# One step of a hybrid encoder layer on one core: the second value pair formed plainly, token squares moved back, roots spread in steps, and sliding-window attention fed from the last gate product

## The chip, the core and the metric

The kernel runs on 1 core of one Trainium2 chip. The metric is device time in microseconds (us), the median of several runs. TensorE (PE) does the matmuls, VectorE (DVE), ScalarE (ACT) and GpSimd (POOL) the elementwise work, and SyncE (SP) issues most of the DMAs. Each engine takes its instructions in the order in which the program lists them.

## The reference, cut to what matters

One layer is computed for 1024 prompt frames and 64 sample frames, here side by side as 1088 columns of 1024 features. With `xn = rms_norm(x)`:

```
rq, rk, rv, rg, sq, sk, sv, ga, gb = split(xn @ w_in)
q, k = rope(rq), rope(rk) / 16                       # 4 heads of 256
for chunk of 64:                                     # retention
    s = (q @ k.T) * decay;  o = s @ v + (q @ state) * q_dec
    state = state * gamma**64 + (k * k_dec).T @ v
a = (rms_norm(o) * silu(rg)) @ w_ret_out
p = softmax(sq @ sk.T / 8 + bias, with a sink)       # 16 heads of 64, window 192
b = (p @ sv) @ w_swa_out
x += (sigmoid(ga) * a + sigmoid(gb) * b) @ w_mix_out
x += cross_attention(rms_norm(x), memory keys and values)
x += (silu(hn @ w_gate) * (hn @ w_up)) @ w_down      # hn = rms_norm(x)
y = rms_norm(x)
```

Everything is float32. A product of two float32 matrices is formed in three matmuls of a reduced float type (`fp32r`): high times high, high times low, low times high. So each operand is split into a high part (ACT casts it, L125) and a low part (DVE subtracts, L126).

## The kernel before, in words

**Projection stage (`project_phase`).** The columns of `w_in` are handled in pairs of 256. The 1024x1088 operand is cut into four quarters B11, B12, B21, B22 (features by tokens), and a pair of weight blocks likewise into a11, a12, a21, a22. `strassen` forms the pair's result in 7 products, P1, P2, P6, P5, P7, P3, P4 in this order, with the operands B11, B21, T2, T1, T3, B22, T4, where T1 to T4 are differences of the quarters. `plain` and `plain_columns` form it in 8 products of the quarters themselves. A product is 24 matmuls of 128x272 columns (`multiply`, L209 to L212). It fills one of three PSUM bank pairs (`pq`), which come round in turn, and a bank pair is free again when its result has been read: by ACT (`u1`, L273, or a copy, L644) or by DVE (`u2`, `u3`, `u5`, L270; the result `stage`, L646). `weight_ops` forms the seven weight operands of a pair from two raw tiles; POOL does its sums (L186 to L193), for the second pair DVE. The weight operands go round in five buffers (`wq`).

**The start.** The first value pair is formed by `plain`, because T1 to T4 do not exist yet. The second value pair is formed by `strassen`, whose T operands DVE and ACT prepare meanwhile (`start_phase`, L484 to L502). Then come keys and queries of head 0, `rotated(w_k, 0)` and `rotated(w_q, 0)`: each result is turned by the rotary table `rope` on DVE (L677 to L683). `token_squares` loads x once more in 16 tiles `xsq` through four buffers (L513), squares them on ACT (L514) and adds them up on DVE (L516). The buffers of `rope` and `xsq` lie where the start's tiles (`early`, `w`) lay.

**Retention beside it.** From `rotated(w_k, 1)` on, one step of the generator `retention_steps` is put behind every product (`product`, `step`). The fourth step forms the token roots (L525 and the chain from L307), a later one spreads them over all partitions (`spread_roots`: nine small matmuls L536 into two banks, three ACT copies L538, all in one step). After that each head takes 25 steps. The pieces wait on each other in PE's order (`in_order`).

**Gates and memory keys.** Twelve gate pairs follow: four of `w_ga`, four of `w_rg`, four of `w_gb`. The first three lie beside the last retention steps. From the fourth on steps of `memory_phase` lie behind each pair.

**Sliding-window attention (SWA, `mix_phase`, `swa`).** 17 chunks of 64 tokens, each in two halves of 8 heads. For a half: `scores` (4 matmuls, L1100), the softmax on DVE and ACT (L1110 to L1126) and POOL (L1128), `turn` (transposes of the probabilities, L1143 and L1151, and a copy by ACT, L1145, and one by DVE, L1153) and `weigh` (4 full and 4 tail matmuls, L1166 and L1171). Step i holds `weigh` of half i-1, `scores` of half i+2, `turn` of half i, and then pieces from `filler`: memory values of heads 2 and 3 (8 pieces), then the product with `w_ret_out` in 8 rows of blocks by 3 column chunks of 384, 384 and 320 (48 pieces of 12 matmuls, L152 to L154). The product's operands `ret` are the gated retention outputs; they are loaded from `d_gate` into the tiles `swin` and split (L125, L126). All of this stage's inputs are loaded when the last gate product has been issued, and `ret` of all three column chunks is split at the stage's beginning:

```
head, (c0, n) = [], CH[0]
...
for t, groups in zip(self.chunk, (((0, 1), (4, 5), (6,)), ((7,), (2, 3)))):
...
operands(head[:5], *CH[0], first)
...
operands(fetch(*CH[t + 1]), *CH[t + 1], (self.max_done, self.exp_done))
```

**What sets the order.** A scheduler puts the instructions of each engine in order; `issue_after` and `in_order` keep an instruction behind another in that order. An engine does not pass over an instruction that waits, and SP does not pass over a DMA that waits.

Of the kernel before, what the change touches and what calls it, by code (L numbers as in the profile page):

```python
# [11 lines left out]
F32 = mybir.dt.float32  # L12
# [4 lines left out]
PSUM = bass.MemoryType.PSUM  # L17
# [93 lines left out]
class Kernel:  # L111
# [57 lines left out]
    def weight_ops(self, raws, n=512, skip=(), by=None):  # L169
# [13 lines left out]
        tt = (by or nc.gpsimd).tensor_tensor  # L183
# [8 lines left out]
        self.ready = self.last_cast, self.last_low  # L192
# [229 lines left out]
    def start_phase(self, ctx):  # L422
# [57 lines left out]
        with tc.issue_after(behind[0]), tc.issue_after(behind[1]):  # L480
            self.second = self.weight_ops(self.load_raws([io["w_v"][2 + i] for i in range(2)]), by=nc.vector)
# [5 lines left out]
        with tc.issue_after(self.ready[0]), tc.issue_after(self.ready[1]):  # L487
# [14 lines left out]
        self.sums_done = self.last_low  # L502
# [27 lines left out]
    def spread_roots(self):  # L530

        for c0, n in ((0, 512), (512, 512), (1024, SMP)):
# [5 lines left out]
            self.nc.scalar.copy(self.rstd[:, c0:c0 + n], pb[:, :n])  # L538

# [74 lines left out]
    def project_phase(self):  # L614
        nc, tc, io = self.nc, self.tc, self.io
        with ExitStack() as ctx:
# [108 lines left out]
            first = self.second  # L725
            sctx.close()
            stage, long, count = *self.stage_tiles(), [0]
            with ExitStack() as rctx:
# [20 lines left out]
                for m in (0, 2, 4):  # L749
# [6 lines left out]
            steps = [0, 1, 2, 2, 2, 3, 3, 2, 0]  # L756
            for idx, w, act in ((1, "w_ga", AF.Sigmoid), (0, "w_rg", AF.Silu), (2, "w_gb", AF.Sigmoid)):
                for m in range(6 if idx == 1 else 0, KT, 2):
# [7 lines left out]
            raws = [self.unit_raw(io["w_mv"][2, i], 4, 256) for i in range(2)]  # L766
            self.values_loaded = self.loaded
            self.value_units = [self.unit_parts(raw, 4, 256) for raw in raws]
# [10 lines left out]
    def retention_steps(self):  # L779
# [6 lines left out]
        self.spread_roots()  # L786
        yield
# [36 lines left out]
    def retention(self, h):  # L824
# [107 lines left out]
        yield  # L932
        pss = self.bank("psss")
# [73 lines left out]

# [29 lines left out]
    def swa(self, ctx, fill):  # L1037
        nc, tc, io = self.nc, self.tc, self.io
        if True:
# [4 lines left out]
            flat = [t.rearrange("p a b -> p (a b)") for t in self.ring_tiles(0, KT, "swin", F32)]  # L1044
# [7 lines left out]
            self.lds += [t[:, i * 384:(i + 1) * 384] for t in (flat[6], flat[3]) for i in range(5)]  # L1052
            self.chunk = [flat[6][:, :5 * 384], flat[3][:, :3 * 384]]
            with tc.high_priority():
                def tokens(dst, i, cache):
                    self.load(dst[:, :SEQ], self.d_skv[i, :, :SEQ])
                    self.load(dst[:, SEQ:SEQ + P], io[cache])
                    ins = self.load(dst[:, SEQ + P:], self.d_skv[i, :, SEQ:])
                    return ins

                tokens(kT, 0, "ckT")
                self.load_queries(qTs, 0)
            with tc.high_priority(), tc.issue_after(self.values_loaded):
                self.bias_loaded = self.load(bias, self.d_bias)
# [67 lines left out]
            def turn(c, hf):  # L1132
                ks, j0, nk = keys(c)
                wide = nk == NKEY
                if hf == 0:
                    tail = [values(ks + P), values(ks - 64)] if wide else None
                    live[c] = [values(ks + 64) if wide and i else values(ks) for i in range(2)], tail
                t = live.pop((c, hf))
                n = min(P, nk)
                pp = pw.tile([P, 512], F32, tag="pt0", name="pp")  # L1140
# [3 lines left out]
                pT = sw.tile([P, 512], F32, tag="pT0", bufs=2, name="pT")  # L1144
                nc.scalar.copy(pT[:n, :], pp[:n, :])  # L1145
                rT = None
# [729 lines left out]
```

## Time and profile before

| | |
|---|---|
| median of 3 runs | 2233.99 us (2232.12 to 2236.03) |
| profiled execution, its own time | 2237.74 us |
| its span from first to last instruction | 2235.7 us |
| mean granted TensorE clock | 0.989 |
| busy: PE, DVE, ACT, POOL | 2166.8, 1605.8, 881.7, 703.6 us |

The page of the profile gives busy times of the engines over the span; "windows" give the same for a stretch of it, with the TensorE clock that was granted there (1.00 is full speed); the chain and the waits name what released an instruction that waited. Start times in the timeline are from the span's start. "x24" behind a row counts instructions; a float32 matmul that is not fp32r counts twice.

### The profile page before, as it was taken

How to read it: one execution, taken by the hardware profiler on the slowest of the kernel's cores; microseconds unless marked ns; L12 is line 12 of the kernel's file. 1: busy time of each engine (PE TensorE's matmuls, PEld its weight loads, DVE VectorE, ACT ScalarE, POOL GpSimd, SP SyncE). 2: the span in 40 equal slices, each digit the busy share in tenths (PEclk: the TensorE clock that was granted, in tenths of full speed). 3: DMA queues.
4: the chain of work that ended last, by engine and by line, in shares of the span. 5: the costliest groups of instructions: out<-in, count | busy, mean ns of one | idle time of the engine just before them, and what ended most of it. 6: DMA issues, size and time to landing. Idle time of an engine off the chain costs nothing.

```text
span 2235.7 us, 42154 instructions
## 1 busy us (share of the span) xinstructions
PE 2166.8 (97%) x16620; PEld 2117.3 (95%) x16620; DVE 1605.8 (72%) x2697; ACT 881.7 (39%) x1897; POOL 703.6 (31%) x522
## 2 busy tenths in 40 slices
PE   9899999999999999999999999999999999999987
PEld 8899999999999997889999998999999999999987
DVE  7888878667688667885455555659777776779787
ACT  6334343436444356553133333324223222335433
POOL 0223535253254112220000000015555555434561
PEclk9999999999999999999999999999999999999999
DMA  6423433344444566326443112422342333476332
GB/s 213 138 98 118 143 118 123 112 146 124 156 142 166 158 237 207 115 71 210 129 153 106 56 48 65 134 85 84 132 135 91 102 116 94 129 246 202 119 120 81
DMA packets 160456, 291.90 MB, mean 131 GB/s; under 512 B 21539, under 2 KB 89059, under 8 KB 160131
## 3 DMA queue, kind: packets, MB, share of 16 engines
q1 hardware_dynamic: 151122, 263.97, 36.8%
q0 software_dynamic: 5104, 17.44, 2.1%
q10 hardware_dynamic: 4032, 7.80, 1.0%
q8 instruction: 131, 2.15, 0.4%
q14 instruction: 67, 0.54, 0.1%
HBM read 197.99 MB, written 91.95 MB: 130 GB/s over the span
## 4 chain that ended last, share of the span: by engine, by line
PE 74%; DVE 10%; DMA 6%; POOL 3%; issue 3%; ACT 3%; SPq 0%; DVEq 0%; ACTq 0%; POOLq 0%
PE pq L209 14%; PE pq L212 14%; PE pq L210 13%; PE pd L152 7%; PE pd L153 7%; PE pd L154 7%; DVE wq L126 3%; PE pss L1100 1%; DVE T L126 1%; DMA hl<-d_op 1%; DVE B L126 1%; DMA xsq<-xT 1%; PE pout L1166 1%; ACT wq L125 1%; POOL raw L189 1%
## 5 line engine op out<-in xcount | busy, mean ns | idle before, releaser
L126 DVE TENSOR_TENSOR wq<-raw,wq 128x512 fp32r<-128x512 f32 (+1 forms) x505 | 459.7, 915 | 154.5 <-ACT wq L125 152.2
L125 ACT CAST wq<-raw 128x512 fp32r<-128x512 f32 (+1 forms) x505 | 305.2, 613 | 602.5 <-PE pq L212 248.3
L209 PE MATMUL pq<-T,wq 128*128 128x272 f32 x1832 | 505.3, 293 | 20.1 <-DVE stage L646 7.8
L210 PE MATMUL pq<-T,wq 128*128 128x272 f32 x1832 | 499.8, 289 | 0.8 <-DVE T L126 0.7
L209 PE MATMUL pq<-B,wq 128*128 128x272 f32 x1526 | 419.3, 292 | 0.5 <-DVE u L270 0.5
L210 PE MATMUL pq<-B,wq 128*128 128x272 f32 x1526 | 414.9, 289 | 0.9 <-DVE B L126 0.9
L212 PE MATMUL pq<-T,wq 128*128 128x272 f32 x1832 | 380.7, 289 | 0.8 <-DVE wq L126 0.8
L186 POOL TENSOR_TENSOR raw<-raw 128x512 f32<-128x512 f32 (+1 forms) x58 | 81.6, 1406 | 939.7 <-DVE rs_r L309 485.9
L209 PEld LDWEIGHTS pq<-T,wq 128*128 128x128 f32 x1832 | 347.6, 190 | 23.3 <-issue 9.0
L210 PEld LDWEIGHTS pq<-T,wq 128*128 128x128 f32 x1832 | 350.9, 192 | 1.5 <-DVE T L126 1.5
L212 PE MATMUL pq<-B,wq 128*128 128x272 f32 x1526 | 316.6, 288 | 0.0
L210 PEld LDWEIGHTS pq<-B,wq 128*128 128x128 f32 x1526 | 291.4, 191 | 1.3 <-DVE B L126 1.3
L209 PEld LDWEIGHTS pq<-B,wq 128*128 128x128 f32 x1526 | 288.6, 189 | 1.4 <-ACT wq L125 0.7
L212 PEld LDWEIGHTS pq<-T,wq 128*128 128x128 f32 x1832 | 286.2, 189 | 1.1 <-DVE wq L126 1.0
L212 PEld LDWEIGHTS pq<-B,wq 128*128 128x128 f32 x1526 | 237.6, 189 | 0.0
L270 DVE TENSOR_TENSOR u<-pq,u 128x544 f32<-128x544 f32 x177 | 127.0, 718 | 79.1 <-PE pq L212 78.3
L189 POOL TENSOR_TENSOR raw<-raw 128x512 f32<-128x512 f32 (+1 forms) x58 | 83.1, 1432 | 117.5 <-DVE wq L126 117.5
L646 DVE TENSOR_TENSOR stage<-pq,u 128x544 f32<-128x544 f32 x112 | 80.1, 716 | 43.0 <-PE pq L212 22.8
L1128 POOL TENSOR_TENSOR t<-t,den 128x768 f32<-128x768 f32 (+2 forms) x34 | 47.7, 1403 | 137.8 <-DVE den L1126 61.1
L193 POOL TENSOR_TENSOR raw<-raw 128x512 f32<-128x512 f32 (+1 forms) x58 | 85.6, 1476 | 16.1 <-DVE wq L126 12.5
L187 POOL TENSOR_TENSOR raw<-raw 128x512 f32<-128x512 f32 (+1 forms) x58 | 83.8, 1444 | 3.7
L1658 POOL TENSOR_TENSOR y<-u,y 128x544 f32<-128x544 f32 x38 | 62.1, 1647 | 49.7 <-DVE y L1656 29.3
(404 smaller groups left out, 4762.5 us busy)
## 6 DMA issues: line engine op xcount, KB each, us to landing
hl<-d_op SPq DMA_DIRECT2D x84, 272.0 KB, 4.0
d_op<-stage SPq DMA_DIRECT2D x44, 272.0 KB, 2.2
d_op<-ht SPq DMA_DIRECT2D x44, 272.0 KB, 4.0
raw<-w_gate SPq DMA_DIRECT2D x22, 512.0 KB, 3.5
raw<-w_up SPq DMA_DIRECT2D x22, 512.0 KB, 4.7
raw<-w_down SPq DMA_DIRECT2D x16, 512.0 KB, 3.9
d_qkv<-stage SPq DMA_DIRECT2D x28, 272.0 KB, 2.4
d_gate<-stage ACTq DMA_DIRECT2D x28, 272.0 KB, 2.5
```

The lines of the kernel that those rows point to most:

```text
L125: self.last_cast = self.nc.scalar.copy(hi, src).ins
L126: self.last_low = self.nc.vector.tensor_tensor(out=lo, in0=src, in1=hi.bitcast(F32), op=ALU.subtract).ins
L152: mm(ps, wh, xh, start=start, stop=False)
L153: mm(ps, wh, xl, start=False, stop=False)
L154: self.last_mm = mm(ps, wl, xh, start=False, stop=stop).ins
L187: tt(out=a21, in0=a21, in1=a22, op=add)
L189: tt(out=a11, in0=a22, in1=a11, op=sub)
L193: self.last_sum = tt(out=a12, in0=a12, in1=a11, op=sub).ins
L209: mm(ps[:, c, :HC], w[:, 0, ks], x[:, 0, cs], start=start, stop=False)
L210: mm(ps[:, c, :HC], w[:, 0, ks], x[:, 1, cs], start=False, stop=False)
L212: self.last_mm = mm(ps[:, c, :HC], w[:, 1, ks], x[:, 0, c * HC:(c + 1) * HC], start=False, stop=stop).ins
L270: add = lambda out, a, b: nc.vector.tensor_tensor(out=out, in0=a, in1=b, op=ALU.add)
```

## The change

1. **Second value pair.** Its weights are split plainly (`plain_weights`, 4 operands and no sums) and `plain_columns` forms it in 8 products, before the start's tiles are given up; its results go through `early` and not through `stage`.
2. **Squares later.** `token_squares` now comes behind the last cast and the last low part of T4, and its buffers become free only after the second pair.
3. **Roots in steps.** `spread_roots` yields after each of its three pieces, and retention's small sample part has one yield more, so that retention has 118 steps where it had 112. All four `w_ga` pairs now lie beside retention.
4. **SWA inputs behind the last gate pair's products.** `refill` calls `swa_inputs` after each product of the last `w_gb` pair: as soon as an operand's place is free, keys, queries, bias and the first 384 columns of the gated retention output are loaded, and these are split into `ret`, in the places of B21, T2, T3 and B22. Raw weights of the memory values are loaded there too.
5. **Other columns.** The 16 tiles of the other two column chunks are fetched into the places of the first ones, and split two at a time, at each piece of `filler`. The three first rows of blocks of `w_ret_out` go together (`lead=3`, before 2), and the outputs of `filler` go round in 4 places until the last of these tiles is split (before 12).
6. **Weighing.** `turn` writes both halves of a chunk into one tile (`tall`, `rest`, one buffer each), and `weigh` of a chunk is one set of 8 matmuls of 256 columns, at every second step, where it was two sets of 8 matmuls of 128 columns.
7. **PSUM.** The banks of the transposes get a pool of their own, ahead of the output's and the scores': transposes, output and scores now lie in the first, second and third bank pair of the projection, where it was output, scores and transposes.

```diff
-            self.second = self.weight_ops(self.load_raws([io["w_v"][2 + i] for i in range(2)]), by=nc.vector)
+            self.second = self.plain_weights(self.load_raws([io["w_v"][2 + i] for i in range(2)]))
...
-        self.sums_done = self.last_low
+        self.sums_done = self.last_cast, self.last_low
...
             self.nc.scalar.copy(self.rstd[:, c0:c0 + n], pb[:, :n])
+            yield
...
             values(first, 0, self.plain)
-            first = self.second
+            values(self.second, 1, self.plain_columns)
             sctx.close()
-            stage, long, count = *self.stage_tiles(), [0]
+            stage, long, count = *self.stage_tiles(), [4]
...
-                values(first, 1)
                 rotated(pair("w_k", 0), 0, 1)
-                with tc.issue_after(self.sums_done):
+                with tc.issue_after(self.sums_done[0]), tc.issue_after(self.sums_done[1]):
                     self.token_squares()
...
-                for m in (0, 2, 4):
+                for m in (0, 2, 4, 6):
                     gate_columns(1, "w_ga", AF.Sigmoid, m)
...
+                    if (idx, m) == (2, KT - 2):
+                        self.refill = self.swa_inputs(mp)
...
+        def split(name, ks):
+            ring, slots = self.slots[name]
+            for k, slot in zip(ks, slots):
+                t = self.rets[k] = self.rings[ring].tile(f"ret{k}", slot=slot)
+                a = dict(self.columns)[k]
+                self.split(a[:, :n], t[:, 0, c0:c0 + n], t[:, 1, c0:c0 + n])
...
+            if name == "B11":
...
+                kT = swin(0)[:, :KC]
+                self.tokens(kT, 0, "ckT")
...
+                columns(swin(6), ((0, 1), (4, 5), (6,)))
+            elif name == "T2":
+                split("B21", (0, 1))
+            elif name == "T1":
+                self.load(swin(2)[:, :NPAIR * NKEY].rearrange("p (a b) -> p a b", b=NKEY), self.d_bias)
+                columns(swin(3), ((7,), (2, 3)))
+                split("T2", (4, 5))
+            elif name == "B22":
+                self.value_units = [self.unit_parts(raw, 4, 256) for raw in raws]
+                split("T3", (6, 7))
+            elif name == "T4":
+                split("B22", (2, 3))
...
         nc.vector.tensor_scalar(kv[:SMP, 1, :], pv[:SMP, 0, :], self.rtok[:SMP, 8:], None, ALU.mult)
         yield
+        yield
...
-            self.po, self.pw = (ctx.enter_context(self.tc.tile_pool(name=n, bufs=1, reuse_waits="tile", space=PSUM))
-                                for n in ("pout", "pw"))
+            self.pt, self.po, self.pw = (ctx.enter_context(self.tc.tile_pool(name=n, bufs=1, reuse_waits="tile", space=PSUM))
+                                         for n in ("pturn", "pout", "pw"))
...
-                        self.last_mm = mm(po[rows[v], i, at], full[i][:n, rows[v]], pT[:n, j * P:(j + 1) * P],
-                                          start=True, stop=rT is None).ins
+                        self.last_mm = mm(po[rows[v], i, :2 * P], full[i][:n, rows[v]], row(tall[:n, 2 * v + i]),
+                                          start=True, stop=rest is None).ins
...
-                if i > 0:
-                    self.in_order(lambda: weigh(*halves[i - 1]))
+                if i > 0 and i % 2 == 0:
+                    self.in_order(lambda: weigh(i // 2 - 1))
...
-            for m, u, (c0, n) in self.m_major(units, CH, tail=1, lead=2):
+            for m, u, (c0, n) in self.m_major(units, CH, tail=1, lead=3):
...
                 for ps in self.pieces(u, rets, c0, n):
+                    if left:
+                        operands(2)
```

**Where instructions move.** The first place is DVE at the end of the second value pair and the beginning of `rotated(w_k, 0)`. `pq` is a product's result, `u` a partial sum of it, `stage` a result, `T_302` and `T_303` (after: `T_289` and `T_290`) are T4, `xsq` a tile of squares, `rope` the rotary table, and `wq<-raw` the low part of a weight operand. Before:

```order
L500 SCALAR_TENSOR_TENSOR xg_115<-xg_115,gains 128x544 x2
L500 SCALAR_TENSOR_TENSOR xg_116<-xg_116,gains 128x544 x2
L126 TENSOR_TENSOR T_302<-xg_115,T_302 128x544 x2
L126 TENSOR_TENSOR T_303<-xg_116,T_303 128x544
L270 TENSOR_TENSOR u_531<-pq,u_530 128x544
L126 TENSOR_TENSOR T_303<-xg_116,T_303 128x544
L516 TENSOR_TENSOR rstd<-rstd,xsq 128x544
L126 TENSOR_TENSOR wq<-raw,wq 128x512
L646 TENSOR_TENSOR stage_522<-pq,u_529 128x544
L646 TENSOR_TENSOR stage_522<-pq,u_532 128x544 x2
```

After, from the end of T4 on:

```order
L126 TENSOR_TENSOR T_290<-xg_116,T_290 128x544
L126 TENSOR_TENSOR wq<-raw,wq 128x512 x4
L646 TENSOR_TENSOR stage_714<-pq,u_749 128x544
L126 TENSOR_TENSOR wq<-raw,wq 128x512
L678 TENSOR_TENSOR stage_713<-stage_714,rope 128x544
L269 TENSOR_TENSOR u_750<-pq,u_749 128x544
L679 TENSOR_TENSOR stage_714<-stage_714,rope 128x544
L515 TENSOR_TENSOR rstd<-rstd,xsq 128x544
L269 TENSOR_TENSOR u_752<-pq,u_750 128x544
L515 TENSOR_TENSOR rstd<-rstd,xsq 128x544 x2
L126 TENSOR_TENSOR wq<-raw,wq 128x512 x2
L269 TENSOR_TENSOR u_751<-pq,u_750 128x544
```

No result of the second pair stands among the T operands any more, and a row that reads `rope` now stands ahead of the readings of the key product's banks, with the squares between them.

The second place is DVE in `rotated(w_q, 0)`, around its P2, which is the row `stage<-pq,u_1043` in both. Before:

```order
L126 TENSOR_TENSOR wq<-raw,wq 128x512
L646 TENSOR_TENSOR stage_523<-pq,u_1043 128x544
L270 TENSOR_TENSOR u_1044<-pq,u_1043 128x544
L678 TENSOR_TENSOR stage_522<-stage_523,rope 128x544
L126 TENSOR_TENSOR wq<-raw,wq 128x512
L679 TENSOR_TENSOR stage_523<-stage_523,rope 128x544
L270 TENSOR_TENSOR u_1046<-pq,u_1044 128x544
```

After:

```order
L515 TENSOR_TENSOR rstd<-rstd,xsq 128x544
L269 TENSOR_TENSOR u_1044<-pq,u_1043 128x544
L683 TENSOR_TENSOR stage_713<-stage_713 128x544
L515 TENSOR_TENSOR rstd<-rstd,xsq 128x544
L126 TENSOR_TENSOR wq<-raw,wq 128x512
L269 TENSOR_TENSOR u_1046<-pq,u_1044 128x544
L646 TENSOR_TENSOR stage_714<-pq,u_1043 128x544
```

The reading of P2's bank moved from ahead of the readings of P6 and P5 (`u_1044`, `u_1046`) to behind both, with squares among them.

The third place is ACT where SWA begins; `pT` is the copy of the transposed probabilities, `ret` the operands of the product with `w_ret_out`. Before:

```order
L1145 COPY pT<-pp 64x512
L125 CAST wq<-raw 128x512 x4
L1122 ACTIVATE t,den<-t,nm 128x128 x4
L1124 ACTIVATE es<-es 128x4
L125 CAST ret_9663<-swin_9628 128x320
L125 CAST ret_9664<-swin_9626 128x320
L125 CAST ret_9667<-swin_9632 128x320
L125 CAST ret_9668<-swin_9632 128x320
L125 CAST ret_9669<-swin_9632 128x320
L125 CAST ret_9670<-swin_9632 128x320
L125 CAST ret_9665<-swin_9632 128x320
L125 CAST ret_9666<-swin_9629 128x320
```

After:

```order
L1203 COPY pT<-pp 64x4x128
L1133 COPY swin_9672<-pd 128x128
L125 CAST wq<-raw 128x512 x2
L1177 ACTIVATE t,den<-t,nm 128x128 x4
L1179 ACTIVATE es<-es 128x4
L125 CAST ret_9489<-swin_9430 128x384
L125 CAST ret_9492<-swin_9430 128x384
L1203 COPY pT<-pp 64x4x128
```

The run of eight casts between one half's exponentials and the next copy has become a pair.

More of the change, by code (lines that the diff above doesn't have):

```diff
@@ L755, in project_phase @@
             memory = self.memory_phase(mp)
-            steps = [0, 1, 2, 2, 2, 3, 3, 2, 0]
-            for idx, w, act in ((1, "w_ga", AF.Sigmoid), (0, "w_rg", AF.Silu), (2, "w_gb", AF.Sigmoid)):
-                for m in range(6 if idx == 1 else 0, KT, 2):
+            steps = [1, 2, 2, 2, 3, 3, 2, 0]
+            for idx, w, act in ((0, "w_rg", AF.Silu), (2, "w_gb", AF.Sigmoid)):
+                for m in range(0, KT, 2):
+                    if (idx, m) == (2, KT - 2):
+                        self.refill = self.swa_inputs(mp)
                     with tc.issue_after(gate_columns(idx, w, act, m)):
@@ L785, in retention_steps @@
             yield
-        self.spread_roots()
-        yield
+        yield from self.spread_roots()
         for h in range(H):
@@ L1042, in swa @@
             mm = nc.tensor.matmul
-            flat = [t.rearrange("p a b -> p (a b)") for t in self.ring_tiles(0, KT, "swin", F32)]
+            for i in range(KT):
+                if i not in self.swin:
+                    self.swin[i] = self.rings[0].tile(f"swin{i}", F32, slot=(self.rings[0].next + i) % KT)
+            flat = [self.swin[i].rearrange("p a b -> p (a b)") for i in range(KT)]
             kT, vT = flat[0][:, :KC], flat[5][:, 64:64 + KC]
@@ L1051, in swa @@
             self.lds = [flat[2][:, NPAIR * NKEY:][:, :384], flat[0][:, KC + 3 * P:][:, :384]]
[L1052 to L1064, printed above, removed]
+            self.lds += [flat[3][:, i * 384:(i + 1) * 384] for i in (3, 4)]
+            with tc.high_priority(), tc.issue_after(self.raws_loaded):
+                self.tokens(vT, 1, "cvT")
+                self.load_rows(qTs[0], 2, 2)
             def keep():
@@ L1202, in swa @@
                         keep()
-            self.in_order(lambda: weigh(*halves[n - 1]))
+            self.in_order(lambda: weigh(n // 2 - 1))
             for pieces in next(fill):
@@ L1263, in filler @@
                     us = self.value_units
-                    first = self.max_done, self.exp_done
                 else:
-                    part = lambda i: self.unit_parts(raws[i // 2][:, i % 2 * 512:][:, :512], 2, 256)
-                    last = lambda: (self.last_cast, self.last_low)
                     with tc.issue_after(self.last_gate):
-                        us = sum((part(i) for i in range(3)), [])
-                    with tc.issue_after(last()[0]), tc.issue_after(last()[1]):
-                        operands(head[:5], *CH[0], first)
-                    with tc.issue_after(last()[0]), tc.issue_after(last()[1]):
-                        us += part(3)
-                    operands(head[5:], *CH[0], last())
-                    us = us[:4], us[4:]
+                        us = [self.unit_parts(raw, 4, 256) for raw in self.raws]
                 for t in range(2):
```

125 lines of the change are left out of this document (68 added, 57 removed).

## Prediction

> **What bounds the kernel now.** I read the page first, then the table of stages (windows), then PE's waits, and for the places the change touches the timeline. The page's first line and the stages that matter (length, then busy us and count of PE, weight loads, DVE, ACT, POOL, then PE's granted clock):
>
> ```profile
> PE 2166.8 (97%) x16620; PEld 2117.3 (95%) x16620; DVE 1605.8 (72%) x2697; ACT 881.7 (39%) x1897; POOL 703.6 (31%) x522
> 33.60:69.10 35.50, 25.84 (x171) 24.69 (x170) 33.63 (x49) 16.24 (x28) 5.50 (x4) 0.86 0.49 162
> 69.10:114.00 44.90, 42.78 (x337) 42.30 (x337) 37.18 (x52) 15.37 (x27) 11.26 (x7) 1.00 0.44 140
> 142.70:150.50 7.80, 7.80 (x51) 7.80 (x51) 7.15 (x12) 1.37 (x4) 0.00 (x0) 0.78 0.33 121
> 150.50:595.00 444.50, 434.14 (x3419) 425.19 (x3417) 340.21 (x609) 191.09 (x411) 174.17 (x151) 0.99 0.39 124
> 595.00:799.20 204.20, 204.20 (x1643) 204.13 (x1643) 148.41 (x199) 85.49 (x145) 76.00 (x62) 1.00 0.49 160
> 799.20:820.50 21.30, 21.27 (x170) 21.05 (x168) 11.86 (x18) 7.63 (x13) 4.11 (x5) 1.00 0.89 310
> 820.50:836.40 15.90, 13.99 (x121) 13.25 (x121) 11.89 (x30) 12.52 (x37) 1.43 (x4) 1.00 0.81 269
> 836.40:883.00 46.60, 40.55 (x292) 34.47 (x290) 35.21 (x90) 27.38 (x99) 10.38 (x8) 0.89 0.72 229
> ```
>
> PE is the bound; a gain is an idle stretch that goes, a low clock that goes, or matmuls that go. Before SWA's steady part there are three such places: the second value pair (33.6 to 69.1: 9.7 idle, clock 0.86, while DVE is busy 33.63 of 35.50), the roots, and the beginning of SWA (820.5 to 883: 1.9 and 6.1 idle, clock 0.89). Retention (150.5 to 595) has 10.4 idle. From 595 to 820.5, through the gates, PE has no gap worth the name, so nothing is to be had there. PE's waits say who ended the idle time (total us, times, longest):
>
> ```profile
> PE pq L209 <- DVE stage L646: 7.8, 3, 5.7
> PE po L152 <- DVE state L899: 3.3, 2, 2.4
> PE pb L536 <- ACT rstd L538: 3.2, 1, 3.2
> PE pout L1166 <- ACT pT L1145: 3.0, 1, 3.0
> PE pd L152 <- ACT swin L1284: 2.6, 1, 2.6
> PE pss L152 <- DVE kt L857: 2.5, 1, 2.5
> PE psss L935 <- DVE kvs L929: 2.3, 1, 2.3
> PE pb L979 <- ACT ret_o L969: 2.0, 1, 2.0
> PE pd L153 <- DVE wq L126: 1.1, 1, 1.1
> PE pss L1100 <- DVE stage L646: 0.8, 1, 0.8
> ```
>
> **Part 1: second pair, squares, first keys and queries.** A product's price comes from a stretch that holds one; the timeline rows are the pair's first matmul, its worst wait, and the first matmul of `rotated(w_k, 1)`:
>
> ```profile
> 814.30:817.32 3.02, 3.02 (x27) 3.02 (x26) 2.59 (x4) 0.83 (x2) 0.00 (x0) 1.00 1.03 368
> 33.65 0.29 PE L209 MATMUL pq<-B,wq 128*128 128x272 f32 x1
> 64.03 0.57 PE L209 MATMUL pq<-T,wq 128*128 128x272 f32 x1 [5.67 <-DVE stage L646]
> 114.00 0.29 PE L209 MATMUL pq<-B,wq 128*128 128x272 f32 x1
> ```
>
> A product is 3.02 us. Before, 21 products (7, 7 and 7) took 114.00 - 33.65 = 80.35 us. Now there are 22, one more at +3.02: 66.4 us without a wait, so 100.1, a gain of 13.9 at most. The second pair itself should run freely: its four weight operands need no sums, the quarters exist already, ACT reads its banks, and the T operands are due only with P6 of the keys, about 64. So the wait of 5.67 goes. What is late next is DVE's queue behind it. These rows are the loads behind the first pair's stores, the first square on ACT, the median landing of the stores and of the `xsq` loads, and DVE at full rate:
>
> ```profile
> 37.54 0.42 SPq L119 DMA_DIRECT2D rope<-c_rope  x1
> 38.01 2.15 SPq L119 DMA_DIRECT2D xsq<-xT  x4
> 46.28 0.66 ACT L514 ACTIVATE rstd<-xsq 128x544 f32<-128x544 f32 x1 [5.55 <-DMA xsq<-xT]
> xsq<-xT SPq DMA_DIRECT2D x16, 272.0 KB, 4.0
> d_qkv<-early SPq DMA_DIRECT2D x4, 272.0 KB, 2.4
> 39.61 5.16 DVE L126 TENSOR_TENSOR T<-xg,T 128x544 fp32r<-128x544 f32 x8
> ```
>
> `rope` and `xsq` lie over `early`, so on SP they now stand behind the second pair's last store: 33.65 + 8 x 3.02 = 57.8, a copy by ACT (0.6, as the copy in part 4) and two issues (0.4 each), 2.4 to land, so about 62. Before, the first square ran 8.3 us after its load was issued; so `rope` and squares are there at about 70. A row that reads `rope` stands in DVE's queue ahead of the keys' partial sums, and all the squares are still to come. From it to the reading of P2's bank in `rotated(w_q, 0)` the order has 39 instructions; at 5.16 / 8 = 0.645 us that is 25.2, so 95.2, and about 3 us of waiting for the fifth `xsq` tile, whose load stands behind a weight load that waits for DVE: 98. P7 needs this bank at 57.8 + 11 x 3.02 = 91.0. So PE waits about 7 there. Such gaps also cost clock: 0.14 x 35.5 = 5 us for the two large ones before, so 2 for this one. Gain: 13.9 - 7 - 2 = **5 us**. Ends: 13.9 if DVE keeps up, 0 if it waits twice as long. The clock row at 142.7 bears on a rule: in the Trainium skill, "TensorE: Matmul & The Clock Gate", Part 1: The HAM clock gate, PE falls to half clock only after an idle window of about 3.4 us. By that rule the gaps of under 3.4 us below would cost no clock, and the sum would be about 5 us smaller (1.7 in part 2, 3 in part 4); the trace disagrees, with 0.78 right behind a gap of 3.17.
>
> **Part 2: the roots.** The wait, in the timeline:
>
> ```profile
> 142.29 0.43 PE L536 MATMUL pb<-ident,rtok 64*128 64x64 f32 x2 [3.17 <-ACT rstd L538]
> ```
>
> The third piece waits for a bank that ACT empties; with a product between the pieces it doesn't. That gives 3.17, and 0.22 x 7.8 = 1.7 of clock: 4.9, taken as **4.5**; ends 0 and 4.9. The squares' last tiles land before this, since the roots come 18 products after the second pair.
>
> **Part 3: retention.** The additional yield puts a product between `kvs` and its matmul: 2.3 gone. Its other waits (2.4, 2.5, 2.0, and 0.9 within the 3.3) depend on which product each step meets, and every step now meets another one; I take them as they are: **2.5 us**, ends +10 (none left) and -8 (as many again). The three later spreads of 118 steps still end inside the 119 products beside them, and the fourth `w_ga` pair is only moved past pool boundaries.
>
> **Part 4: SWA's beginning.** ACT's rows show the reason of the 2.6 and 3.0 waits, casts of `ret` in bursts ahead of what PE waits for; the next two show the load of the second `w_ret_out` rows and the cast that waited for it, the last a whole step of SWA later on:
>
> ```profile
> 836.41 2.98 ACT L125 CAST ret<-swin 128x384 fp32r<-128x384 f32 x7
> 847.02 2.96 ACT L125 CAST ret<-swin 128x320 fp32r<-128x320 f32 x8
> 849.89 0.57 ACT L1145 COPY pT<-pp 64x512 f32<-64x512 f32 x1
> 836.49 0.42 SPq L119 DMA_DIRECT2D raw<-w_ret_out  x1
> 841.88 1.14 ACT L125 CAST wq<-raw 128x512 fp32r<-128x512 f32 x2 [0.58 <-DMA raw<-w_ret_out]
> 878.61:883.00 4.39, 4.39 (x44) 3.63 (x43) 3.07 (x7) 2.37 (x10) 1.47 (x1) 1.00 0.29 87
> ```
>
> The 24 splits cost the same, but eight move under the last gate pair, where DVE is busy 11.86 and ACT 7.63 of 21.30 and PE never waits, and sixteen go out in pairs. At 2.98 / 7 = 0.43 on ACT and no more than 0.645 on DVE the eight add 3.4 and 5.2 us there: covered; without cover each would hold up the reading of a bank by 0.645, 5 us in all. The 0.8 goes too, since the scores' banks are now those of P7, not of P4, which is read last. All of it is worth 1.9 + 6.1 idle and 0.11 x 46.6 = 5.1 of clock: 13. But in the new order a pair of `wq` casts stands ahead of the third half's exponentials, and the raw tile of the third rows is free only when the first rows are split. A load to its cast took 841.88 - 836.49 = 5.4 us, a step of PE lasts 4.4: I leave 3 us of wait and 2 of clock. Gain **8 us**; ends 2 and 13.
>
> **Part 5: weighing.** PE's groups in SWA's steady part (883 to 1005, 25 halves):
>
> ```profile
> L1166 PE MATMUL pout<-pT,swin 128*64 128x128 f32 x200 | 16.4, 285 | 0.0
> L1171 PE MATMUL pout<-rT,swin 64*64 64x128 f32 x200 | 11.2, 294 | 0.0
> L1100 PE MATMUL pss<-swin,swin 64*128 64x192 f32 x192 | 22.1, 349 | 0.0
> ```
>
> Columns are the same, instructions half. Per instruction: 82 ns at 128 columns (L1166), 115 at 192 (L1100), so 0.52 ns a column and 16 ns that don't depend on columns. A chunk loses 16 instructions: 0.26 us, times 17 is 4.4, taken as **4 us**; ends 0 (time goes by columns alone) and 8 (twice the fixed part). The single buffers cost nothing: the next `turn` stands behind `weigh` on PE anyway.
>
> **The sum.** 5 + 4.5 + 2.5 + 8 + 4 = 24 us. Against the profiled execution's 2237.74 (span 2235.7 and 2 around it) that is 2213.7. The median of the runs lies 3.75 below that execution, so the forecast is 2233.99 - 24 = **2210**.
>
> **The rivals.**
> *All waits go.* DVE keeps up because `rope` lands sooner, and the third weight load is in time: 9 and 5 us more, 38 in all, 2196. For it: DVE saves the second pair's sums and readings. Against: its queue is full as it is, 37.18 of 44.90.
> *The waits move.* Part 1 gives 0, part 4 gives 3, part 5 gives 1, with the roots' 4.5: 8.5, so 2225.5. For it: an engine's queue is in order, and new rows stand ahead of the readings in two of the three places shown.
> *Weighing gives nothing.* the 16 ns are hidden behind the matmul before, and time goes by columns alone: 0 instead of 4, so 2214. The groups speak against it with their 16 ns. It is what the Trainium skill says in "TensorE: Matmul & The Clock Gate", Back-to-back issue gap: a fixed part of about 2.5 ns for a matmul, by which 272 fewer would save 0.7 us; no row here shows a matmul with so small a part.
> *Nothing is left.* The wait in part 1 is 14 and SWA's beginning stays as it is: within 0.2%, about 2231.
> *Slower, by retention.* Every step behind the roots meets another product than before. In a product beside which DVE turns keys, a step's operand is 2.4 late (`state`, `kt`), and a gap costs about 1 of clock (0.01 x 444.5 over five gaps). At ten of the 16 blocks that is 34 us, against 21.5 from the other parts: +12.5, so 2246.5. It decides from eight blocks on. Against it: before, three blocks had such a gap.
>
> **How the numbers follow.** Chances: the forecast 0.48, all waits go 0.15, the waits move 0.16, weighing gives nothing 0.07, nothing is left 0.06, slower by retention 0.08. Faster by over 0.2% (4.5 us, about what a measurement of this kernel tells from no change): 0.48 + 0.15 + 0.16 + 0.07 = 0.86; same 0.06; slower 0.08. The range takes in the forecast's own spread and the two rivals around it, 2196 and 2225.5, with a little for their sizes: 2194 to 2228.
>
> **What would show it.** In the profile after: the second pair's 192 matmuls without a gap, at full clock, ending near 58; a wait of P7 in `rotated(w_q, 0)` for DVE's `stage`, and `rotated(w_k, 1)` beginning near 109; no wait of L537's spread; no `kvs` wait; scores right behind the last gate product, one wait of a few us for a `w_ret_out` load, and no low clock from 840 on the old scale; a weighing group of 100 instructions under 16.4 - 1 us. Wrong would be: more than eight waits of over 2 us in retention; or DVE's rows for `xsq` standing so late that the roots wait for them.

## The result, and the profile after

| | before | after |
|---|---|---|
| median of 4 runs | 2235.01 us | 2207.93 us (2206.57 to 2209.00) |
| ratio, 95% interval | | 0.9876 (0.9861 to 0.9890) |
| profiled execution | 2237.74 us | 2208.46 us |
| its span | 2235.7 us | 2206.7 us |

The change made the kernel 27.1 us faster; 24 were forecast. (Of the executions of the kernel before beside the first experiments below, one took 10017 us; it counts in no ratio.) The page's first line on the changed kernel:

```profile
PE 2156.8 (98%) x16388; PEld 2103.6 (95%) x16388; DVE 1591.5 (72%) x2683; ACT 882.6 (40%) x1899; POOL 713.9 (32%) x522
```

Its windows over the stages that answer to those of before, with the same columns:

```profile
33.15:57.30 24.15, 24.15 (x195) 24.15 (x194) 20.74 (x29) 10.89 (x19) 12.77 (x4) 1.00 0.22 83
57.30:104.30 47.00, 44.23 (x338) 43.82 (x337) 36.71 (x51) 19.73 (x33) 11.05 (x7) 0.96 0.63 210
...
118.00:142.70 24.70, 24.70 (x185) 24.45 (x185) 22.76 (x53) 7.84 (x15) 7.37 (x4) 0.93 0.32 101
142.70:585.00 442.30, 437.31 (x3459) 427.41 (x3458) 338.64 (x617) 195.17 (x418) 173.95 (x151) 1.00 0.40 129
...
782.60:803.80 21.20, 21.20 (x172) 21.05 (x170) 14.63 (x24) 10.31 (x20) 3.68 (x4) 1.00 0.82 277
803.80:820.00 16.20, 14.89 (x126) 13.72 (x125) 10.12 (x28) 11.19 (x33) 2.47 (x5) 1.00 0.80 252
820.00:866.00 46.00, 37.94 (x256) 30.60 (x258) 39.11 (x91) 25.96 (x97) 10.15 (x7) 0.96 0.68 209
```

Its largest waits of PE from 33 to 866 us (total us, times, longest):

```profile
PE pout L1219 <- ACT pT L1203: 2.9, 3, 1.3
PE pq L208 <- DVE stage L646: 2.7, 4, 1.2
PE pss L152 <- DVE kt L917: 2.6, 4, 1.0
...
PE pq L208 <- DVE u L269: 2.4, 1, 2.4
...
PE pd L1131 <- ACT swin L1133: 1.7, 1, 1.7
PE pd L152 <- ACT swin L1314: 1.7, 1, 1.7
...
PE pss L1155 <- DVE t L1165: 1.6, 1, 1.6
```

The second pair (33.15 to 57.30) now runs without a gap. The waits for `kvs` (2.3), `ret_o` (2.0) and the roots' bank (3.2) are gone, and none of those shown is longer than 2.4. But SWA's beginning (803.8 to 866) still has 1.3 + 8.1 us of idle PE, where the same work had 8.0 before: its long waits (3.0 and 2.6) have become more and shorter ones (the longest 1.7). PE's timeline at the places that the prediction named:

```profile
33.15 0.29 PE L208 MATMUL pq<-B,wq 128*128 128x272 f32 x1
...
93.62 0.40 PE L208 MATMUL pq<-T,wq 128*128 128x272 f32 x1 [2.36 <-DVE u L269]
...
104.30 0.29 PE L208 MATMUL pq<-B,wq 128*128 128x272 f32 x1
...
129.00 1.05 PE L535 MATMUL pb<-ident,rtok 128*128 128x128 f32 x8
...
136.92 0.43 PE L535 MATMUL pb<-ident,rtok 64*128 64x64 f32 x2
```

With the starts of the same work in both profiled executions the 29 us of the span come from these stretches. "Idle" is the stretch less PE's busy time. "Low clock" is what half clock cost: half of the busy time in it (how the stretches at half clock are found stands further down).

| stretch | before | after | idle before, after | low clock before, after (to 2195 us) |
|---|---|---|---|---|
| start to the token roots | 126.06 | 116.35 | 13.2, 4.3 | 3.8, 1.7 |
| to the last gate pair | 673.16 | 666.25 | 13.5, 7.1 | 5.1, 1.7 |
| to SWA's first scores | 22.07 | 21.18 | 0.8, 0.0 | 0, 0 |
| first 9 halves of SWA | 58.29 | 55.12 | 7.2, 8.0 | 4.8, 1.7 |
| next 22 halves | 111.70 | 108.67 | 1.2, 1.6 | 0, 0 |
| to the first product with `swa` | 37.38 | 35.83 | 1.1, 0.0 | 0, 0 |
| to the root of the mixing stage | 177.90 | 176.13 | 1.3, 0.0 | 0, 0 |
| to the last matmul | 1021.64 | 1020.02 | 23.2, 21.7 | 3.1, 3.2 |

### The profile page after: what moved, and what is told of

The parts are those of the page before. It is cut to its first block, busy times and chain, and to the rows that moved or that the text cites. A ratio compares the mean times of both kernels' runs of the same rounds, so it can differ in the third digit from the quotient of the medians.

```text
span 2206.7 us, 41635 instructions
## 1 busy us (share of the span) xinstructions
PE 2156.8 (98%) x16388; PEld 2103.6 (95%) x16388; DVE 1591.5 (72%) x2683; ACT 882.6 (40%) x1899; POOL 713.9 (32%) x522
## 4 chain that ended last, share of the span: by engine, by line
PE 71%; DVE 13%; DMA 7%; ACT 3%; issue 3%; POOL 3%; SPq 0%; POOLq 0%; DVEq 0%; ACTq 0%
PE pq L208 13%; PE pq L211 13%; PE pq L209 12%; PE pd L152 7%; PE pd L154 7%; PE pd L153 7%; DVE wq L126 3%; DMA raw<-w_down 1%; ACT wq L125 1%; DVE B L126 1%; DMA raw<-w_rg 1%; DVE stage L646 1%; PE pss L1155 1%; POOL raw L189 1%; DVE T L126 1%
## 5 line engine op out<-in xcount | busy, mean ns | idle before, releaser
L126 DVE TENSOR_TENSOR wq<-raw,wq 128x512 fp32r<-128x512 f32 (+1 forms) x498 | 448.5, 905 | 168.3 <-ACT wq L125 166.2
L125 ACT CAST wq<-raw 128x512 fp32r<-128x512 f32 (+1 forms) x498 | 300.1, 612 | 576.1 <-PE pq L211 213.4
L208 PE MATMUL pq<-T,wq 128*128 128x272 f32 x1800 | 495.5, 293 | 12.9 <-ACT wq L125 4.9
L209 PE MATMUL pq<-T,wq 128*128 128x272 f32 x1800 | 489.7, 289 | 0.0
L208 PE MATMUL pq<-B,wq 128*128 128x272 f32 x1550 | 424.3, 292 | 1.2 <-DVE stage L646 1.2
L209 PE MATMUL pq<-B,wq 128*128 128x272 f32 x1550 | 419.9, 288 | 0.0
L186 POOL TENSOR_TENSOR raw<-raw 128x512 f32<-128x512 f32 (+1 forms) x58 | 86.6, 1493 | 928.8 <-DVE rs_r L308 483.3
L211 PE MATMUL pq<-T,wq 128*128 128x272 f32 x1800 | 373.8, 289 | 0.8 <-DVE wq L126 0.8
L208 PEld LDWEIGHTS pq<-T,wq 128*128 128x128 f32 x1800 | 340.6, 189 | 16.6 <-ACT wq L125 5.8
L209 PEld LDWEIGHTS pq<-T,wq 128*128 128x128 f32 x1800 | 343.8, 191 | 0.0
L211 PE MATMUL pq<-B,wq 128*128 128x272 f32 x1550 | 320.3, 287 | 0.0
L209 PEld LDWEIGHTS pq<-B,wq 128*128 128x128 f32 x1550 | 294.5, 190 | 0.1
L208 PEld LDWEIGHTS pq<-B,wq 128*128 128x128 f32 x1550 | 291.6, 188 | 2.5 <-ACT mraw L555 1.4
L211 PEld LDWEIGHTS pq<-T,wq 128*128 128x128 f32 x1800 | 280.6, 189 | 1.1 <-DVE wq L126 1.0
L211 PEld LDWEIGHTS pq<-B,wq 128*128 128x128 f32 x1550 | 240.2, 188 | 0.0
L269 DVE TENSOR_TENSOR u<-pq,u 128x544 f32<-128x544 f32 x174 | 124.8, 718 | 71.6 <-PE pq L211 70.9
L189 POOL TENSOR_TENSOR raw<-raw 128x512 f32<-128x512 f32 (+1 forms) x58 | 84.0, 1448 | 112.5 <-DVE wq L126 108.3
L646 DVE TENSOR_TENSOR stage<-pq,u 128x544 f32<-128x544 f32 x108 | 77.3, 716 | 32.3 <-PE pq L211 21.5
L192 POOL TENSOR_TENSOR raw<-raw 128x512 f32<-128x512 f32 (+1 forms) x58 | 85.3, 1471 | 15.7 <-DVE wq L126 12.2
L187 POOL TENSOR_TENSOR raw<-raw 128x512 f32<-128x512 f32 (+1 forms) x58 | 85.6, 1475 | 3.7
```

What stands on the lines that cost most here:

```text
L125: self.last_cast = self.nc.scalar.copy(hi, src).ins
L126: self.last_low = self.nc.vector.tensor_tensor(out=lo, in0=src, in1=hi.bitcast(F32), op=ALU.subtract).ins
L186: tt(out=a11, in0=a11, in1=a21, op=sub)
L189: tt(out=a11, in0=a22, in1=a11, op=sub)
L208: mm(ps[:, c, :HC], w[:, 0, ks], x[:, 0, cs], start=start, stop=False)
L209: mm(ps[:, c, :HC], w[:, 0, ks], x[:, 1, cs], start=False, stop=False)
```

## The experiments

All medians are of 4 or 5 runs, with the kernel before run 9 times beside them (medians 2234.11, 2233.31 and 2233.45 us in the three groups). Intervals are about 0.0013 to each side of a ratio, some 3 us, so two versions of the changed kernel can be told apart by their times only from some 4 us on. What is smaller has to come from the stretches of the profiled executions, of which there is one for each kernel.

**Part 1 alone.** Parts are counted here as in the prediction. The kernel before, with the squares behind the last work on T4, and with

```
-self.second = self.weight_ops(self.load_raws(...), by=nc.vector)
+self.second = self.plain_weights(self.load_raws(...))
...
+values(self.second, 1, self.plain_columns)
```

> The kernel before with the first part of the change alone: the second value pair plainly in 8 products, the squares behind T4. Forecast: 5 us faster than before (14 of waits and clock go, 7 of wait and 2 of clock come back at P7 of rotated(w_q, 0)), so 2230. From the trace of the changed kernel, where the same stretch is 9.2 us shorter: 2226, with one wait of about 2.4 us at P7 of rotated(w_q, 0) and no other over 1 us between the second pair and rotated(w_k, 1). If part of the 9.2 us comes from the other parts of the change (the roots' steps stand close behind), less than 7 us remain. Wait of the roots' third spread: about 3.2 us as before, since it is not touched.

Measured: 2225.27 us, ratio 0.9966 (0.9953 to 0.9979). From the second pair's first matmul to `rotated(w_k, 1)` its trace has 71.76 us where before had 80.35: 8.6 less. Its waits:

```profile
PE psss L934 <- DVE kvs L928: 3.7, 1, 3.7
...
PE pb L536 <- ACT rstd L538: 2.7, 1, 2.7
...
PE pq L209 <- DVE u L270: 2.4, 1, 2.4
```

Part 1 brings 8 to 9 us by itself, more than the 5 forecast. The roots' wait and that for `kvs` are still there (2.7 and 3.7 us, before 3.2 and 2.3).

**Parts 1 to 3, with the old SWA stage.** The kernel of part 1, and the yields, the fourth `w_ga` pair and `steps` as in the change.

> The kernel before with parts 1 to 3 of the change (second pair, roots in steps, retention's additional yield and the fourth w_ga pair beside it), with the old sliding-window stage. Forecast: 5 + 4.5 + 2.5 = 12 us faster than before, 2222. From the trace of the changed kernel: 9.2 us up to rotated(w_k, 1) and 6.9 from there to the last gate pair, 16.1, so 2218, and the sliding-window stage then brings the other 10 of the change's 26. Rival: parts 2 and 3 bring nothing beside part 1 (the run with the spread in one step was no slower that can be measured): 2225, as with part 1 alone.

Measured: 2219.24 us, ratio 0.9937 (0.9924 to 0.9949), 14.1 us below before. So parts 2 and 3 bring 5 to 6 us beside part 1, and the SWA stage the remaining 11 to 13 of the change's 25 to 27. All that PE waits for in retention there (142 to 778 us; it was 10.4 before):

```profile
PE pss L152 <- DVE kt L856: 3.3, 4, 1.4
PE po L152 <- DVE state L898: 0.8, 1, 0.8
PE pkvs L948 <- DVE ret_t L982: 0.2, 1, 0.2
```

**The spread in one step.** The changed kernel, with `yield` in `spread_roots` moved out of the loop.

> The changed kernel with the three pieces of the root spread in one step again. Forecast: the third piece waits 3.2 us for its bank, and 1.7 us of low clock follow: 4.9 us slower than the changed kernel, 2213. Rival, clock in fixed windows: the low clock depends on where the gap falls, and the changed kernel has a low stretch of 3.4 us behind the 18 root matmuls already, so 1.5 to 4.9 us. Rival, covered: no wait comes back, 0.

Measured: 2209.49 us, ratio 0.9893 (0.9879 to 0.9907); the changed kernel beside it 2209.17. PE's waits from 115 to 165 us in this kernel:

```profile
PE pb L535 <- ACT rstd L537: 2.4, 1, 2.4
PE pss L152 <- DVE kt L917: 0.3, 1, 0.3
```

and in the changed kernel, from 116 to 165:

```profile
PE pss L152 <- DVE kt L917: 1.0, 1, 1.0
PE pq L208 <- DVE stage L646: 0.9, 1, 0.9
```

The bank's wait is back with 2.4, but the changed kernel has 1.6 more of two other waits, both for DVE, 8 and 16 us behind its third piece. DVE is busy almost without a break there (the stretch of this kernel, then the busy time of PE, weight loads and DVE):

```profile
115.28:165.00 49.72, 47.07 (x380) 46.59 (x379) 48.05 (x97) 19.82 (x42) 12.90 (x8) 1.00 0.37 118
```

With DVE busy 48.05 of 49.72, it seems that PE waits for it at one place or another; that is read from this one trace. Up to the last gate pair this kernel needs 779.06 us with nothing lost to low clock, the changed one 782.60 with 3.4 lost. Beside the yield of part 3 the steps are worth nothing that shows. One thing more came in at the other end: the first scores wait for the reading of the last gate product's result, which stands on DVE behind two early splits. DVE's rows:

```profile
801.83 1.02 DVE L126 TENSOR_TENSOR ret<-swin,ret 128x384 fp32r<-128x384 f32 x2
802.77 0.72 DVE L646 TENSOR_TENSOR stage<-pq,u 128x544 f32<-128x544 f32 x1
```

and PE's first scores:

```profile
803.54 0.55 PE L1155 MATMUL pss<-swin,swin 64*128 64x64 f32 x6 [3.23 <-DVE stage L646]
```

The changed kernel has the same rows on DVE without that wait, so its scores do not stand in that bank; here they seem to. Why the place of a bank moved with a yield was not settled.

**The additional yield taken out.**

> The changed kernel without the additional yield in retention's small sample part. Forecast: the wait for kvs of 2.3 us comes back and the others stay, so 2211 against 2208.5. Rival, alignment: every later step stands beside another product, and the waits for kt, state and ret_o (4.8 us in all in the changed kernel, 8.0 in the kernel before) take other sizes; then kvs need not wait at all, and the time lies anywhere from 2205 to 2216.

Measured: 2208.69 us, ratio 0.9890 (0.9876 to 0.9903): no difference. `kvs` is waited for 0.2, not 2.3. The spread's yields move every later step by two products against before, the sample part's yield by one more for each head that is done. So this kernel, the one with the spread in one step and the changed one pair steps and products in three ways; all three have lost retention's waits of over 2 us, and the kernel with part 1 alone, which pairs them as before, has not. So the pairing fits as the cause, and either edit shifts it enough: with the steps there, the yield in the sample part is not needed, and without them it suffices.

**Weighing by halves.** The changed kernel, with the loops of `weigh` run for each half:

```
+for h in range(2):
+    at = slice(h * P, (h + 1) * P)
...
-mm(po[rows[v], i, :2 * P], full[i][:n, rows[v]], row(tall[:n, 2 * v + i]), ...)
+mm(po[rows[v], i, at], full[i][:n, rows[v]], row(tall[:n, 2 * v + i])[:, at], ...)
```

> The changed kernel with each weighing matmul of 256 columns cut into two of 128, at the same place and on the same operands (272 more matmuls, same columns). Forecast, 16 ns for an instruction: 4.4 us slower than the changed kernel, 2212. Trace of the changed kernel, whole stretch: 5.4 us, 2213. A fixed part of 2.5 ns for a matmul, which the Trainium skill states: 0.7 us, 2208.6, no difference that can be measured.

Measured: 2209.40 us, ratio 0.9891 (0.9877 to 0.9905). The time alone would suit 2.5 ns for a matmul, which the Trainium skill ("TensorE: Matmul & The Clock Gate", Back-to-back issue gap) states. The 22 halves of the steady part say otherwise. Their window in this kernel (the stretch, then PE's busy time):

```profile
857.13:967.58 110.45, 110.05 (x983) 92.52 (x983) 91.48 (x228) 66.49 (x252) 33.89 (x22) 1.00 0.35 108
```

in the changed kernel:

```profile
858.90:967.57 108.67, 107.08 (x807) 86.46 (x807) 92.25 (x228) 66.05 (x252) 33.95 (x22) 1.00 0.35 110
```

and in the kernel before:

```profile
879.58:991.28 111.70, 110.54 (x987) 92.76 (x984) 92.07 (x223) 63.77 (x246) 32.32 (x22) 1.00 0.33 101
```

176 more matmuls of the same columns cost 110.05 - 107.08 = 2.97 us of PE: 17 ns each. The change drops 256 (the profiles count 512 before and 256 after; two of the 17 chunks have no tail, so the forecast's 272 is too many), and that is 4.3 us. It doesn't reach the end in full: the stretch is only 1.8 us shorter, because PE idles 1.6 in it and 0.4 by halves. Most of the difference is one wait of 1.3 for ACT's copy `pT`. So part of the work saved comes back as waiting.

**SWA's beginning.** Three kernels with one line each: the eight early splits all behind T4 (`splits_late`), `lead=2` for `lead=3` (`lead2`), and the PSUM pools in the old order (`old_banks`).

> The changed kernel with the eight early splits of the retention outputs all behind the last gate product instead of behind four of them. Forecast, the last gate pair covers them: without that cover 8 x 0.43 us on ACT and 8 x 0.4 to 0.65 on DVE stand ahead of the first scores' softmax, so 3 to 5 us slower, 2212 to 2213. Rival, DVE and ACT have time to spare in the first steps: 0 to 1 us. Trace: the first copy of turned probabilities would wait longer, and the low clock at SWA's beginning stand or double.

> The changed kernel with two first rows of blocks of w_ret_out together instead of three. Forecast: the third row's load costs 3 us of wait and 2 of clock at SWA's beginning, which go: 5 us faster, 2203.5. From the changed kernel's trace, in which no wait of PE there is for a w_ret_out load: 0, or a little slower, since the next columns' operands are due four pieces earlier.

> The changed kernel with the PSUM pools of sliding-window attention in the old order (output, scores, transposes). Forecast: the 0.8 us wait of the first scores for the reading of the last gate product's bank comes back, and nothing else: 2209.3, not to be told from 2208.5 by the time, but to be seen in PE's waits. Rival: the first transposes or weighing then wait for that bank later instead: 0.

Measured: 2207.34 (ratio 0.9886, 0.9873 to 0.9900), 2213.46 (0.9906, 0.9892 to 0.9919) and 2208.50 (0.9886, 0.9873 to 0.9900). Splitting early brings nothing that the time shows, though the profile of the late splits has 4.9 us of low clock in the first 9 halves against 1.7. Three rows together, for which the forecast charged 5 us, are worth 4 to 5 by the medians. The interval with two rows lies clear of the first one of the changed kernel (0.9861 to 0.9890), but overlaps with the second (0.9876 to 0.9912). The profile goes the same way. With two rows the 22 halves take 111.55 us, where the changed kernel needs 108.67 and 108.75 in its two profiles:

```profile
860.63:972.18 111.55, 109.00 (x807) 86.99 (x807) 91.38 (x228) 66.26 (x252) 33.12 (x22) 0.98 0.34 108
```

The next columns' operands come too late, and 3.4 us more are lost to low clock in the 31 halves. The wait that is new:

```profile
PE pd L152 <- ACT ret L125: 1.7, 1, 1.7
```

With the old banks the scores' wait is 2.6 and not 0.8, since early splits now stand ahead of that reading; the time doesn't show it.

**Rows moved from DVE to POOL.** DVE is busy at both places where PE still waits, so two kernels move its additions of the squares (`squares_pool`, below) or the later 16 low parts of `ret` (`low_pool`, likewise), and one both (`both_pool`):

```
-nc.vector.tensor_tensor(out=acc, in0=acc, in1=x, op=ALU.add)
+nc.gpsimd.tensor_tensor(out=acc, in0=acc, in1=x, op=ALU.add)
```

> The changed kernel with the 14 additions of the token squares on POOL instead of DVE. DVE's queue, which has no idle time from the landing of the rotary table to P7 of rotated(w_q, 0), loses 10 rows of 0.65 us ahead of the reading that P7 waits for: the wait of 2.4 us goes, and with it 1.7 us of low clock where there was any: 2.4 to 4.1 us faster than the changed kernel's 2208.5, 2204 to 2206. Rival: POOL's additions take some 1.5 us each and stand ahead of its sums of the weights for rotated(w_q, 0) and rotated(w_k, 1), so that PE waits there for wq instead: 0, or slower by up to 5 us. Rival, first reason of the forecast: what sets the wait is the landing of the rotary table, not the squares: 0.

> The changed kernel with the 16 later low parts of the retention outputs formed on POOL instead of DVE. If DVE bounds SWA's beginning (it is busy 39.1 of the 46 us in which PE waits 8.1), 16 x 0.5 = 8 us leave its queue and most of the waits go: 4 to 7 us faster, 2202 to 2205. If ACT's copies and exponentials set the end of those waits: 0. If POOL, with about 1 us a row and the softmax products in the same queue, is late with them: slower, by up to 16 us.

> The changed kernel with both: the squares' additions and the 16 later low parts of the retention outputs on POOL. If the two places are independent and DVE's queue is what PE waits for in both: 2 to 4 us from each, 2201 to 2204, faster than either kernel. If POOL's rows are late in the first place: 2206 or more.

Measured: 2215.70 (0.9915, 0.9902 to 0.9928), 2205.63 (0.9874, 0.9859 to 0.9890) and 2210.23 (0.9893, 0.9880 to 0.9907). With the squares on POOL the kernel is some 6 us slower, as the rival had it. PE's waits from 33 to 143 us were

```profile
PE pq L208 <- DVE stage L646: 5.7, 4, 2.3
PE pq L211 <- DVE wq L126: 3.6, 1, 3.6
```

POOL's sums of the weights stand behind the additions: those for `rotated(w_q, 0)` end at 87.3, in the changed kernel at 82.3. But DVE has won nothing either. From the row that reads `rope` on, it is as busy with 22 rows in this kernel (first) as with 35 in the changed one:

```profile
68.15:93.00 24.85, 18.94 (x144) 18.54 (x143) 22.64 (x22) 12.40 (x21) 20.49 (x13) 0.90 0.55 186
68.76:93.56 24.80, 22.09 (x174) 21.67 (x172) 24.50 (x35) 12.57 (x21) 6.39 (x4) 1.00 0.63 202
```

POOL is busy 20.49 us there and not 6.39, and many of DVE's rows take 1.7 to 1.9 us instead of 0.7 while it works (more in the last section). With the low parts on POOL the first 9 halves of SWA take 53.06 us, against 55.12 and 56.15 in the two profiles of the changed kernel:

```profile
806.81:859.87 53.06, 47.03 (x337) 39.97 (x336) 41.49 (x92) 35.16 (x119) 21.59 (x24) 0.97 0.73 233
```

This doesn't show DVE as the bound: with the low parts still on DVE, the kernel with the old banks needs 52.61 for the same halves, and all profiles with this SWA stage and three rows lie between 49.8 (`both_pool`) and 57.3 (`splits_late`).

```profile
801.58:854.19 52.61, 45.05 (x336) 38.78 (x336) 40.59 (x98) 32.82 (x114) 10.47 (x10) 1.00 0.74 233
```

The medians don't tell the kernel with the low parts on POOL from the changed one, and ACT's copies hold most of the waits that are left in it. No version was clearly faster than the changed kernel.

**The changed kernel again.**

> The changed kernel as it is, as the measure for the three beside it: 2208 us within 1.5. Clock: if the granted clock is judged in fixed windows of time that run freely, the stretches at half clock again last 3.4 us or a multiple, but need not stand at the same places as in the first profile (behind the wait at P7 of rotated(w_q, 0), behind the 18 root matmuls, and at SWA's beginning); if they follow from the kernel alone, they stand at the same three places.

Measured: 2209.17 us, ratio 0.9894 (0.9876 to 0.9912). Half clock stood again behind P7's wait and at SWA's beginning, but not behind the root matmuls. What decides is shown in the last section.

## Why the prediction came out as it did

The sign, the size and the range were right. Of the five terms one was right in size; the others were off in both directions and nearly cancelled, so that the sum came so close is in part luck.

- **Part 1, 5 forecast, 9.2 in the trace, 8 to 9 alone.** The second pair ran without a gap, and P7 of `rotated(w_q, 0)` waited for DVE, as forecast. The size of that wait was off, 7 forecast and 2.4 measured, because the step "P7 needs this bank" failed. These rows are DVE's reading of `rope`, a row of POOL and one of DVE beside it, then DVE's readings of the banks of P6 and of P2:

```profile
68.76 0.73 DVE L678 TENSOR_TENSOR stage<-stage,rope 128x544 f32<-128x544 f32 x1 [3.90 <-DMA rope<-c_rope]
...
76.21 1.81 POOL L187 TENSOR_TENSOR raw<-raw 128x512 f32<-128x512 f32 x1
76.78 1.82 DVE L677 TENSOR_TENSOR stage<-stage,rope 128x544 f32<-128x544 f32 x1
...
92.85 0.71 DVE L269 TENSOR_TENSOR u<-pq,u 128x544 f32<-128x544 f32 x1
...
97.31 0.71 DVE L646 TENSOR_TENSOR stage<-pq,u 128x544 f32<-128x544 f32 x1
```

  P7 began at 93.62, behind the reading of P6's bank and 3.7 us ahead of that of P2's. So it took P6's bank: the bank pairs did not come round strictly in turn here, as the description of the kernel before says they do. P7 needed 34 of the 39 rows counted. The 39th ended at 98.0, just where the forecast had it, but that is luck. `rope` was there 1.2 us earlier than assumed, and the 3 us of waiting for the fifth `xsq` tile did not come: up to 93.5 DVE was idle for 0.3. In their place three rows beside POOL's sums took 1.82, 1.40 and 1.82 us instead of 0.7, and behind P7's start DVE waited 1.2 for a cast.
- **Part 2, 4.5 forecast, about nothing beside part 3.** The wait named did go. The step that failed is that the sum doesn't ask what is late next: DVE is nearly full there, and 1.6 us came back as two other waits. The clock's 1.7 came back behind the root matmuls in the profiled execution.
- **Part 3, 2.5 forecast, 5 to 6 with part 2.** "I take them as they are" was wrong for the other waits: the same shift that freed `kvs` shortened `state` from 3.3 us to 0.8 and took away the 2.0 for `ret_o`, while `kt` kept 2.6 in smaller pieces and 1.3 of small new waits came. Two stretches of low clock went with them. The yield, to which the forecast gave the 2.3 us, was not needed for it. That parts 2 and 3 together come to the forecast's 7.0 (6.9 in the trace) is two errors of opposite sign. The rival of ten late blocks stayed far: no wait of the changed kernel in retention was over 1.1.
- **Part 4, 8 forecast, about 3.** That is 0.9 before the scores and 3.2 in the first 9 halves, less about 1 that the weighing saves there. In the first 9 halves the idle time didn't fall (7.2 to 8.0); what fell was low clock (4.8 to 1.7). As that differs from 0 to 4.9 among the kernels with this stage, the 3 is not well known. The third load's wait, 3 us and 2 of clock, never showed; without the third row the kernel is 4 to 5 us slower by the medians, so this edit had the opposite sign from the one given to it. The early splits, counted as covered and useful, brought nothing that shows.
- **Part 5, 4 forecast, 4.3 of PE's work.** The 16 ns were measured as 17, for 256 matmuls instead of 272. In time it was less, 1.8 of 3.0 in the 22 halves, since PE waits more there. The Trainium skill ("TensorE: Matmul & The Clock Gate", Back-to-back issue gap) has 2.5 ns for a matmul by itself, and that does not hold here. The same section has about 81 ns a matmul of 128 columns in a stream in which each has its own weight load; that agrees with the 82 ns shown with the prediction.
- **Not in the sum:** 1.1 us at the end of SWA and 1.3 at the first products with `swa`, waits of which at most 0.4 is left in any kernel with the new SWA stage. Which edit took them was not tried.

## What to carry to other kernels

Removing a wait pays only as far as the engine that was waited for has time to spare behind it: look at its busy share in the next 50 us before counting the gain, and undo one edit at a time afterwards, since two wrong terms can add up to a right sum. Before moving rows from DVE to POOL, look at how long DVE's other rows take while POOL works. Where a generator's steps lie beside products, shift all of them by one or two and measure, because each wait there belongs to a pairing. A saving of work on PE, measured as busy time, is worth its size only in stretches in which PE does not wait.

## What the runs showed of the hardware

**The clock is judged in fixed windows of 3.41 us.** In 14 profiled executions (before, after and the twelve runs) the granted clock fell to 0.50 74 times ahead of 2195 us: 72 times for 3.41 us or twice that, and twice at 2194.6 and 2194.8 to the end of the program. Within an execution all the starts lie on one grid of 3.413 us, to 0.01 us; the grid's phase differs between executions. Cut along that grid, the changed kernel's windows read (length, PE's busy time first, the clock third from the end):

```profile
91.51:94.92 3.41, 1.30 (x10) 1.30 (x11) 3.32 (x6) 0.84 (x2) 0.00 (x0) 1.00 0.94 335
94.92:98.34 3.42, 3.42 (x17) 3.42 (x17) 2.27 (x4) 1.14 (x2) 0.19 (x1) 0.50 0.99 387
115.41:118.82 3.41, 3.41 (x31) 3.38 (x31) 2.23 (x4) 0.00 (x0) 0.00 (x0) 1.00 0.95 258
118.82:122.24 3.42, 3.42 (x18) 3.42 (x17) 2.75 (x5) 2.42 (x3) 0.70 (x1) 0.50 0.75 286
```

A window with PE busy 1.30 of 3.41 is followed by one at half clock, though the gap in it was only 2.36. Of all windows at full clock in the 14 executions, each of the 51 in which PE was busy less than 44% was followed by half clock; from 44% to 70% it was 16 of some 170, above that 4 of 8600. So a gap of 2.4 us costs 1.7 more or nothing, by where it falls. In the kernel before, the wait of 2.32 for `kvs` lay across a border, and cost nothing:

```profile
460.88:464.29 3.41, 1.98 (x16) 1.76 (x14) 2.97 (x9) 1.02 (x3) 1.94 (x2) 1.00 0.78 249
464.29:467.70 3.41, 2.52 (x21) 2.45 (x22) 3.41 (x8) 1.64 (x4) 0.89 (x1) 1.00 0.49 150
```

The Trainium skill ("TensorE: Matmul & The Clock Gate", Part 1: The HAM clock gate) says that this window runs freely, and the runs agree; that a whole idle window is needed, they do not bear out.

**Matmuls of two columns do not keep the clock up.** All four of the exceptions above 70% are windows that hold the 18 token-root matmuls whole (2.05 us, two columns each), as 115.41 to 118.82 does; no other execution has them whole in one window. Without them PE is busy 1.36 of 3.41 us there, 40%, and that fits the 44% above, so they seem to count as idle time. In the second profile of the changed kernel they lie across a border (118.16), and no low clock follows. That is why the low clock behind the roots could come and go with no change in the program.

**POOL's sums hold up some of DVE's rows.** In the changed kernel DVE forms 269 low parts `wq<-raw` of 128x512 (both operands in SBUF) while POOL does nothing, each in 0.67 to 0.70 us. Of the 204 that have a row of POOL beside them 148 took over 0.9 us, up to 2.9. The 110 rows that read a bank (L269, L646) beside POOL took at most 0.73, as they do without it.
